# The adaLN columns of the last residual's gate, made in the feed-forward loop instead of beside the gate projections

## The chip, the cores and the metric

The kernel runs on one core of a Trainium2 chip, as one program. The metric is the device time of one execution in microseconds (us); where several executions were timed, their median is given. A profiled execution also has a span, from its first to its last instruction.

## The reference

One layer of a diffusion backbone works on 512 latent rows of width 1024, with 256 context rows beside them. The adaLN projection makes six vectors of 1024 values out of the condition `c`; the rest of the layer uses them as shift, scale and gate:

```python
ada = jax.nn.silu(c)[:, None, :] @ w_ada[layer] + b_ada[layer]
sh1, sc1, g1, sh2, sc2, g2 = jnp.split(ada, 6, axis=-1)
...
parts = _split_in(modulate(rms_norm(h_lat, norm1_w[layer]), sh1, sc1) @ w_in[layer])
mix, _ = _mixer(parts, lp, states, latent_conv)
h_lat = h_lat + g1 * mix
h_lat = h_lat + g2 * _swiglu(modulate(rms_norm(h_lat, norm2_w[layer]), sh2, sc2),
                             w_gate[layer], w_up[layer], w_down[layer])
return rms_norm(h_lat, final_norm_w)
```

`_mixer` joins a gated linear attention (GLA, 4 heads) and a state-space branch (SSD, 4 groups), `merged = sigmoid(gate_a) * y_a + sigmoid(gate_b) * y_b`, and multiplies the result by `w_out`. `_swiglu` has an inner width of 2816, that is 22 blocks of 128. All is float32. The gate `g2` is needed only at the very end, when the result of the feed-forward part is added to the residual.

## The kernel before

**Precision and weights.** Each float32 product is made of three matmuls, high x high, high x low and low x high. A weight block of 128 x 1024 values (512 KB) is loaded into one of three `raw` buffers by a transfer that SP issues (`load_raw`, L176), ScalarE copies it into the high half `whi_...` (L188), and VectorE, in some stages GpSimd (POOL), subtracts to get the low half `wlo_...` (L189). The high and the low halves have two buffers each. A raw buffer is free again when the low half is made. A scheduler sets the order of the instructions on each engine when the program is built; the engines then run their own lists in order and wait for each other through semaphores. SP runs no arithmetic: its list is that of the transfers.

**The adaLN columns.** `ada` holds 48 columns of 128 values, eight for each of the six vectors: 0 to 15 are made at the start, 16 to 23 are g1, 24 to 39 sh2 and sc2, 40 to 47 g2. `some_ada` makes the late ones beside other work. Every second call, as long as columns are left, it does two things: it finishes the column before (a matmul of a 128 x 128 block with a column of ones, L336, and a bias added by VectorE, L215) and starts the next (a load of 512 KB into a raw buffer, and on GpSimd a product with the condition, L341, two halvings, L343, and a last addition `apr`, L345). The calls stand in the projections of the GLA heads and, twice per step, in those of the gates.

**The stages in the text.** Before 880 us, the heads and the groups of the SSD. From about 880 to 990 us, the *gate stage*: a loop over the columns 2 to 7 of the merge gates (L927 on) loads and projects `ga_j` and `gb_j`, with `ya_j` read back from memory, while the recurrence of the last SSD group (`ssd_chain`) goes on: E row blocks are read from `cdr` (L829), biased (L830), multiplied by `cb` (L840), its outputs `y` are transposed (`yT`). The tanh of a gate, `tg`, is written to `tdr` by GpSimd's queue (L936). Then the rest of the columns, the row transpose `adaT` (L942), its copy `adT`, written to memory as `adr` by GpSimd's queue (L946) and read back by SP broadcast over the partitions: g1r (L949), sh2 and sc2 (L955). The last projection `pb_3` follows, and with it `merge` (L980 on), which reads `tgm` from `tdr` and for j below 2 `yam` from `ydr`, and adds on GpSimd (L989). The *output projection* (about 1008 to 1050 us) multiplies each `raw_out` by g1r on GpSimd (L187) and splits it. The norm `hn` (L1031, L1032) and its transposes `hT` (L1035) follow, while the first weights of the feed-forward part are split. The *feed-forward loop* (FFN; about 1070 to 1310 us) has 22 steps over the inner blocks, 48 matmuls each for `gate_j` and `up_j`; then w_down, the gate g2r and the last norm.

In the kernel before, `late` holds the columns 16 to 47, and g2r is read from the one `adr` at the start of the loop:

```python
while late or half_done:
    some_ada()
pt = sm_bank("adaT")
nc.tensor.transpose(pt[0:96, 0:P], ada.rearrange("p j t -> p (j t)"), ident)
```

Of the kernel before, what the change touches and what calls it, by code (L numbers as in the profile page):

```python
# [7 lines left out]
F32 = mybir.dt.float32  # L8
# [6 lines left out]
P = 128  # L15
D = 1024
# [113 lines left out]
def hybrid_layer_kernel(ctx: ExitStack, tc: tile.TileContext, x, xc, wts, vec, rows, up, msk, lvl, out):  # L130
    nc = tc.nc
# [10 lines left out]
    dr = ctx.enter_context(tc.tile_pool(name="dr", bufs=1, space=DRAM))  # L142

    def mm_bank(name):
        return ps.tile([P, 512], F32, tag="mm", name=name)

    def sm_bank(name):
        return ps.tile([P, 512], F32, tag="sm", name=name)
# [11 lines left out]
    ident = idt[:, :]  # L160
# [33 lines left out]
    def load_w(key, row=None):  # L194
        if key in ahead:
            return ahead.pop(key)
        nk, ncol = WSHAPE[key]
        nm = "_".join(map(str, key))
        hi = wp.tile([P, nk, ncol], F32R, tag="whi", name="whi_" + nm)
        lo = wp.tile([P, nk, ncol], F32R, tag="wlo", name="wlo_" + nm)  # L200
        return split_w(key, hi, lo, row)
# [9 lines left out]
    ada = cst.tile([P, 48, 2], F32, name="ada")  # L211
# [13 lines left out]
    with tc.tile_pool(name="st", bufs=1) as st:  # L225
# [77 lines left out]
        for i in range(6):  # L303
# [5 lines left out]
            for half in range(2):  # L309
                pt = sm_bank(f"xT_{i}_{half}")  # L310
# [11 lines left out]

    late = list(range(16, 48))
    half_done = []
    loads = [0]

# [137 lines left out]
    for d in range(2):  # L466
        for i in range(6):
            pt = sm_bank(f"pre_{d}_{i}")
# [16 lines left out]
    for b, i0, n in ((0, 0, 4), (1, 4, 2)):  # L485
        pt = sm_bank(f"dtT_{b}")
# [73 lines left out]
    for d in range(2):  # L560
        pt = sm_bank(f"cumT_{d}")
# [379 lines left out]
    pt = sm_bank("adaT")  # L941
# [5 lines left out]
    arow = adr.rearrange("(j t) p -> t j p", t=2)  # L947
# [66 lines left out]
    for i in range(4):  # L1014
# [14 lines left out]
        for half in range(2):  # L1029
# [3 lines left out]
            pt = sm_bank(f"hT_{i}_{half}")  # L1033
# [16 lines left out]
    fp = ctx.enter_context(tc.tile_pool(name="fp", bufs=1))  # L1050
    fH = fp.tile([P, NFF, SEQ], F32R, name="fH")
    fL = fp.tile([P, NFF, SEQ], F32R, name="fL")
    g2r = fp.tile([P, D], F32, name="g2r")
    nc.sync.dma_start(g2r.rearrange("p (j c) -> p j c", c=P), arow[0:1, 40:48, :].to_broadcast([P, 8, P]))
    fnr = fp.tile([P, D], F32, name="fnr")
    nc.sync.dma_start(fnr, rows[0:1, R_FN:R_FN + D].to_broadcast([P, D]))

    for j0, nj in [(0, 2)] + [(j, 1) for j in range(2, NFF)]:
        js = range(j0, j0 + nj)
        ws = {(key, j): load_w((key, j)) for j in js for key in ("gate", "up")}  # L1060
        pts = {(key, j): mm_bank(f"{key}_{j}") for j in js for key in ("gate", "up")}
        for t0, n in (((0, 256), (256, 256)) if nj == 2 else ((0, 512),)):
            tk = slice(t0, t0 + n)
            for kj, (hi, lo) in ws.items():
                for k in range(KD):
                    nc.tensor.matmul(pts[kj][:, tk], hi[:, k, :], h2H[:, k, tk], start=(k == 0), stop=False)  # L1066
                    nc.tensor.matmul(pts[kj][:, tk], hi[:, k, :], h2L[:, k, tk], start=False, stop=False)  # L1067
                    nc.tensor.matmul(pts[kj][:, tk], lo[:, k, :], h2H[:, k, tk], start=False, stop=(k == KD - 1))  # L1068
        for j in js:
            if nj == 2:  # L1070
                f = sml.tile([P, SEQ], F32, tag="snw", name=f"f_{j}", bufs=1)
            else:
                f = fp.tile([P, SEQ], F32, tag="f32", name=f"f_{j}", bufs=2)
            nc.scalar.activation(f, pts["gate", j], AF.Silu)
            nc.vector.tensor_tensor(f, f, pts["up", j], ALU.mult)  # L1075
            nc.scalar.activation(fH[:, j, :], f, AF.Copy)
            nc.vector.tensor_tensor(fL[:, j, :], f, fH[:, j, :].bitcast(F32), ALU.subtract)

    ob = [[(sm_bank if i < 2 else mm_bank)(f"db_{i}_{c}") for c in range(2)] for i in range(4)]
    fHk = [fH[:, k, :] for k in range(NFF)]  # L1080
    fLk = [fL[:, k, :] for k in range(NFF)]
    K0 = NFF - 6
# [119 lines left out]
```

## Time and profile before

| | |
|---|---|
| median of 3 runs | 1442.92 us (1441.3 to 1446.59) |
| profiled execution | 1443.79 us |
| its span | 1442.0 us, mean granted clock of TensorE 0.981 |
| TensorE matmuls busy | 1357.0 us (94% of the span) |
| VectorE busy | 882.6 us (61%) |
| ScalarE busy | 497.1 us (34%) |
| GpSimd busy | 475.3 us (33%) |

The first lines are times of whole executions; the others come from one profiled execution, that is from its span. TensorE is the engine with most work, and the time outside its 94% is either a wait at one of the stages or the start and the end of the kernel. The granted clock is the share of full speed (2.4 GHz) that TensorE was given; half of it, 1.2 GHz, is its other level. The program moves 175.48 MB in 1442.0 us.

### The profile page before, as it was taken

The numbers are of one execution on the slowest core, as the hardware profiler recorded it, in microseconds if no ns is written. First come the engines' busy times: TensorE is split into PE (matmuls) and PEld (weight loads), VectorE is DVE, ScalarE is ACT, GpSimd is POOL, SyncE is SP. The second block draws the span as 40 slices with busy tenths as digits, with TensorE's granted clock in tenths as the row PEclk, the third lists the DMA queues.
The fourth block names the chain that finished last, engine by engine and source line by source line (L and its number), as shares of the span: only waits on it lengthen the run. The fifth ranks groups of instructions, "written<-read, shape, count | busy, mean of one in ns | idle before, by whom it ended". The sixth has DMA issues, their size and how long they took to land.

```text
span 1442.0 us, 19130 instructions
## 1 busy us (share of the span) xinstructions
PE 1357.0 (94%) x7461; PEld 1149.3 (80%) x7461; DVE 882.6 (61%) x1316; ACT 497.1 (34%) x825; POOL 475.3 (33%) x340
## 2 busy tenths in 40 slices
PE   5989999999998999998999999999889999999997
PEld 3788999889888778877877787777678888888886
DVE  4699767573495588559757876785783333333235
ACT  6464333423434132523432342322233322322222
POOL 1346554344423533343353336445740000000001
PEclk9898999999999999999999999999999999999999
DMA  9385424433422432322322233558523222232331
GB/s 370 118 264 148 134 88 128 106 103 111 124 78 66 142 103 89 96 88 88 110 74 88 88 110 102 179 179 283 171 88 97 94 102 91 100 102 88 103 103 72
DMA packets 71354, 175.48 MB, mean 122 GB/s; under 512 B 6368, under 2 KB 22880, under 8 KB 71136
## 3 DMA queue, kind: packets, MB, share of 16 engines
q1 hardware_dynamic: 57056, 161.11, 33.5%
q0 software_dynamic: 13920, 12.78, 3.6%
q8 instruction: 59, 0.97, 0.3%
q10 hardware_dynamic: 288, 0.36, 0.1%
q14 instruction: 31, 0.25, 0.1%
HBM read 159.37 MB, written 14.86 MB: 121 GB/s over the span
## 4 chain that ended last, share of the span: by engine, by line
PE 62%; DVE 16%; DMA 11%; issue 5%; POOL 3%; ACT 2%; SPq 0%; POOLq 0%; DVEq 0%; ACTq 0%
DMA E<-cdr 7%; PE gate L1067 3%; PE gate L1068 3%; PE gate L1066 3%; PE up L1067 3%; PE up L1068 3%; PE up L1066 3%; PE db L206 3%; PE db L204 3%; PE db L205 3%; DVE E L830 2%; PE lv L577 2%; PE pb_pb L716 1%; PE pb_pb L715 1%; PE pb_pb L717 1%
## 5 line engine op out<-in xcount | busy, mean ns | idle before, releaser
L341 POOL TENSOR_TENSOR raw_ada<-raw_ada,cs 128x1024 f32<-128x1024 f32 x32 | 67.6, 2113 | 159.4 <-DMA raw_ada<-in_wts_dram 109.2
L170 POOL TENSOR_TENSOR rr_f<-rv_f,negh 128x1 f32<-128x1 f32 x4 | 2.6, 646 | 355.3 <-DVE rv_f L168 355.3
L830 DVE TENSOR_TENSOR E<-E,ebias 128x512 f32<-128x512 f32 x64 | 66.3, 1038 | 56.2 <-DMA E<-cdr 56.0
L386 PE MATMUL r_z<-whi_z,hH 128*128 128x256 f32 x256 | 74.5, 291 | 5.8 <-DVE cv_x L746 3.5
L343 POOL TENSOR_TENSOR raw_ada<-raw_ada 128x512 f32<-128x512 f32 x64 | 78.5, 1227 | 3.0
L388 PE MATMUL r_z<-whi_z,hL 128*128 128x256 f32 x256 | 73.2, 286 | 0.0
L387 PE MATMUL r_z<-wlo_z,hH 128*128 128x256 f32 x256 | 72.9, 285 | 0.0
L1067 PE MATMUL gate<-h2L,whi_gate 128*128 128x512 f32 (+1 forms) x192 | 72.0, 375 | 0.7 <-DVE h2L L1039 0.7
L1066 PE MATMUL gate<-h2H,whi_gate 128*128 128x512 f32 (+1 forms) x192 | 72.3, 377 | 0.0
L1068 PE MATMUL gate<-h2H,wlo_gate 128*128 128x512 f32 (+1 forms) x192 | 71.9, 374 | 0.0
L189 DVE TENSOR_TENSOR wlo_gate<-raw_gate,whi_gate 128x1024 fp32r<-128x1024 f32 x20 | 24.5, 1225 | 73.8 <-ACT whi_gate L188 73.8
L189 POOL TENSOR_TENSOR wlo_xs<-raw_xs,whi_xs 128x1024 fp32r<-128x1024 f32 x16 | 41.2, 2573 | 74.3 <-ACT whi_xs L188 74.3
L1066 PE MATMUL up<-h2H,whi_up 128*128 128x512 f32 x160 | 62.2, 389 | 0.0
L1067 PE MATMUL up<-h2L,whi_up 128*128 128x512 f32 x160 | 62.2, 389 | 0.0
L1068 PE MATMUL up<-h2H,wlo_up 128*128 128x512 f32 x160 | 62.2, 389 | 0.0
L189 DVE TENSOR_TENSOR wlo_down<-raw_down,whi_down 128x1024 fp32r<-128x1024 f32 x18 | 22.0, 1225 | 62.4 <-ACT whi_down L188 62.3
L833 ACT ACTIVATE E<-E 128x512 f32<-128x512 f32 x32 | 20.2, 632 | 112.0 <-DVE E L832 87.8
L1075 DVE TENSOR_TENSOR f<-f,up 128x512 f32<-128x512 f32 x22 | 15.1, 688 | 69.2 <-PE up L1068 68.5
L386 PE MATMUL r_v<-whi_v,hH 128*128 128x256 f32 x192 | 56.8, 296 | 0.0
L189 POOL TENSOR_TENSOR wlo_z<-raw_z,whi_z 128x1024 fp32r<-128x1024 f32 x16 | 39.7, 2484 | 49.1 <-ACT whi_z L188 39.4
L387 PE MATMUL r_v<-wlo_v,hH 128*128 128x256 f32 x192 | 55.8, 291 | 0.0
L388 PE MATMUL r_v<-whi_v,hL 128*128 128x256 f32 x192 | 55.8, 291 | 0.0
(475 smaller groups left out, 4544.4 us busy)
## 6 DMA issues: line engine op xcount, KB each, us to landing
raw_ada<-in_wts_dram SPq DMA_DIRECT2D x32, 512.0 KB, 4.0
E<-cdr SPq DMA_DIRECT2D x64, 256.0 KB, 3.6
raw_gate<-in_wts_dram SPq DMA_DIRECT2D x22, 512.0 KB, 3.5
raw_up<-in_wts_dram SPq DMA_DIRECT2D x22, 512.0 KB, 3.5
raw_down<-in_wts_dram SPq DMA_DIRECT2D x22, 512.0 KB, 3.5
aw<-in_wts_dram SPq DMA_DIRECT2D x8, 1024.0 KB, 15.5
raw_xs<-in_wts_dram SPq DMA_DIRECT2D x16, 512.0 KB, 3.5
raw_z<-in_wts_dram SPq DMA_DIRECT2D x16, 512.0 KB, 3.5
```

The lines of the kernel that those rows point to most:

```text
L189: (nc.gpsimd if split_pool[0] else nc.vector).tensor_tensor(lo, raw, hi.bitcast(F32), ALU.subtract)
L204: nc.tensor.matmul(out_, aH, bH, start=start, stop=False)
L205: nc.tensor.matmul(out_, aH, bL, start=False, stop=False)
L341: nc.gpsimd.tensor_tensor(raw, raw, cs[:, :, 0:1].to_broadcast([P, KD, P]), ALU.mult)
L343: nc.gpsimd.tensor_tensor(raw[:, 0:n, :], raw[:, 0:n, :], raw[:, n:2 * n, :], ALU.add)
L386: nc.tensor.matmul(o, hH[:, kk, tk], hi[:, k, :], start=st, stop=False, skip_group_check=True)
L387: nc.tensor.matmul(o, hH[:, kk, tk], lo[:, k, :], start=False, stop=False, skip_group_check=True)
L388: nc.tensor.matmul(o, hL[:, kk, tk], hi[:, k, :], start=False, stop=sp, skip_group_check=True)
L830: nc.vector.tensor_tensor(ed, ed, ebias[:, d, n, hh].unsqueeze(2).to_broadcast([P, EH, P]), ALU.add)
L1066: nc.tensor.matmul(pts[kj][:, tk], hi[:, k, :], h2H[:, k, tk], start=(k == 0), stop=False)
L1067: nc.tensor.matmul(pts[kj][:, tk], hi[:, k, :], h2L[:, k, tk], start=False, stop=False)
L1068: nc.tensor.matmul(pts[kj][:, tk], lo[:, k, :], h2H[:, k, tk], start=False, stop=(k == KD - 1))
```

## The change

The columns 40 to 47, those of g2, leave the list that is worked off beside the projections and the gates. The list gets them back ahead of the feed-forward loop, and each step of the loop from j = 2 on makes one call of `some_ada`, so that every second step makes a column. Behind the loop a row transpose of these eight columns alone (16 x 128) is made, copied, written to memory as `adr2` by GpSimd's queue and read back as g2r by SP. The arithmetic is the same.

```diff
@@ -322,7 +322,7 @@
 
 
 
-    late = list(range(16, 48))
+    late = list(range(16, 40))
     half_done = []
     loads = [0]
 
@@ -1050,14 +1050,15 @@
     fp = ctx.enter_context(tc.tile_pool(name="fp", bufs=1))
     fH = fp.tile([P, NFF, SEQ], F32R, name="fH")
     fL = fp.tile([P, NFF, SEQ], F32R, name="fL")
-    g2r = fp.tile([P, D], F32, name="g2r")
-    nc.sync.dma_start(g2r.rearrange("p (j c) -> p j c", c=P), arow[0:1, 40:48, :].to_broadcast([P, 8, P]))
+    late += range(40, 48)
     fnr = fp.tile([P, D], F32, name="fnr")
     nc.sync.dma_start(fnr, rows[0:1, R_FN:R_FN + D].to_broadcast([P, D]))
 
     for j0, nj in [(0, 2)] + [(j, 1) for j in range(2, NFF)]:
         js = range(j0, j0 + nj)
         ws = {(key, j): load_w((key, j)) for j in js for key in ("gate", "up")}
+        if j0 >= 2:
+            some_ada()
         pts = {(key, j): mm_bank(f"{key}_{j}") for j in js for key in ("gate", "up")}
         for t0, n in (((0, 256), (256, 256)) if nj == 2 else ((0, 512),)):
             tk = slice(t0, t0 + n)
@@ -1077,6 +1078,18 @@
             nc.vector.tensor_tensor(fL[:, j, :], f, fH[:, j, :].bitcast(F32), ALU.subtract)
 
     ob = [[(sm_bank if i < 2 else mm_bank)(f"db_{i}_{c}") for c in range(2)] for i in range(4)]
+    while late or half_done:
+        some_ada()
+
+    pt = sm_bank("adaT2")
+    nc.tensor.transpose(pt[0:16, 0:P], ada[:, 40:48, :].rearrange("p j t -> p (j t)"), ident)
+    adT2 = fp.tile([16, P], F32, name="adT2")
+    nc.vector.tensor_copy(adT2, pt[0:16, 0:P])
+    adr2 = dr.tile([16, P], F32, name="adr2")
+    nc.gpsimd.dma_start(adr2, adT2)
+    g2r = fp.tile([P, D], F32, name="g2r")
+    nc.sync.dma_start(g2r.rearrange("p (j c) -> p j c", c=P),
+                      adr2.rearrange("(j t) p -> t j p", t=2)[0:1].to_broadcast([P, 8, P]))
     fHk = [fH[:, k, :] for k in range(NFF)]
     fLk = [fL[:, k, :] for k in range(NFF)]
     K0 = NFF - 6
```

The scheduler places the moved instructions, and so the order on each engine changes at three places. The first is the transfer queue, SP, in the middle of the gate stage, from one raw_gb to the next. `raw_ada` is an adaLN column, `ya` the row block of the first branch, `E` the row blocks of the last SSD group. Before:

```order
L176 DMA raw_gb_4_8478<-in_wts_dram 128x1024
L176 DMA raw_ada_43_8514<-in_wts_dram 128x1024
L929 DMA ya_5_8509<-ydr_1127 128x512
L829 DMA E_3_2_1_1_8150<-cdr_700 128x512
L829 DMA E_3_3_0_0_8209<-cdr_700 128x512
L829 DMA E_3_3_0_1_8212<-cdr_700 128x512
L176 DMA raw_ga_5_8523<-in_wts_dram 128x1024
L176 DMA raw_gb_5_8557<-in_wts_dram 128x1024
```

And with the change, in the same stretch of the program:

```order
L176 DMA raw_gb_5_8520<-in_wts_dram 128x1024
L929 DMA ya_5_8482<-ydr_1127 128x512
L829 DMA E_3_2_1_1_8153<-cdr_700 128x512
L829 DMA E_3_3_0_0_8212<-cdr_700 128x512
L829 DMA E_3_3_0_1_8215<-cdr_700 128x512
L176 DMA raw_ga_6_8555<-in_wts_dram 128x1024
L829 DMA E_3_3_1_0_8220<-cdr_700 128x512
```

The raw_ada in front of ya and the three E is gone, and the weights are loaded one step further ahead: behind the same E stands raw_ga_6 where raw_ga_5 stood.

The second place is the end of the gate stage. On GpSimd (POOL), `adr` is the write of the row transpose, `tdr` that of a tanh, `tgm` the addition in the merge, `raw_out` the product of a weight block with g1r. Before:

```order
L343 TENSOR_TENSOR raw_ada_47_8759<-raw_ada_47_8759 128x256
L345 TENSOR_TENSOR apr_47_8764<-raw_ada_47_8759 128x128
L936 DMA tdr_1128<-tg_7_8710 128x1024
L989 TENSOR_TENSOR tgm_0_0_8829<-tgm_0_0_8829,tgm_0_1_8830 128x512
L946 DMA adr_8773<-adT_8771 96x128
L989 TENSOR_TENSOR tgm_1_0_8854<-tgm_1_0_8854,tgm_1_1_8855 128x512
L187 TENSOR_TENSOR raw_out_0_9025<-raw_out_0_9025,g1r_8775 128x1024
L187 TENSOR_TENSOR raw_out_1_9056<-raw_out_1_9056,g1r_8775 128x1024
L187 TENSOR_TENSOR raw_out_2_9087<-raw_out_2_9087,g1r_8775 128x1024
```

And with the change:

```order
L936 DMA tdr_1128<-tg_6_8584 128x1024
L170 TENSOR_TENSOR rr_y33_8265<-rv_y33_8263,negh_83 128x1
L946 DMA adr_8693<-adT_8691 96x128
L936 DMA tdr_1128<-tg_7_8653 128x1024
L989 TENSOR_TENSOR tgm_0_0_8749<-tgm_0_0_8749,tgm_0_1_8750 128x512
L989 TENSOR_TENSOR tgm_1_0_8774<-tgm_1_0_8774,tgm_1_1_8775 128x512
L187 TENSOR_TENSOR raw_out_0_8945<-raw_out_0_8945,g1r_8695 128x1024
L187 TENSOR_TENSOR raw_out_1_8976<-raw_out_1_8976,g1r_8695 128x1024
```

The write of adr now stands ahead of the last tdr and of tgm_0, where it stood behind both, and the columns' work in front of them is gone. On SP, in the same part of the program, `hres` are four blocks of the residual, 512 KB each. Before:

```order
L176 DMA raw_ada_47_8759<-in_wts_dram 128x1024
L176 DMA raw_pb_3_0_8811<-in_wts_dram 128x1024
L176 DMA raw_pb_3_1_8867<-in_wts_dram 128x1024
L176 DMA raw_pb_3_2_8917<-in_wts_dram 128x1024
L971 DMA hres_0_8795<-in_x_dram 128x1024
L971 DMA hres_1_8796<-in_x_dram 128x1024
L176 DMA raw_pb_3_3_8967<-in_wts_dram 128x1024
L971 DMA hres_2_8797<-in_x_dram 128x1024
L971 DMA hres_3_8798<-in_x_dram 128x1024
L176 DMA raw_out_0_9025<-in_wts_dram 128x1024
L986 DMA yam_1_8858<-ydr_1127 128x512
L176 DMA raw_out_1_9056<-in_wts_dram 128x1024
```

And with the change:

```order
L176 DMA raw_pb_3_2_8837<-in_wts_dram 128x1024
L986 DMA yam_0_8753<-ydr_1127 128x512
L982 DMA tgm_1_0_8774<-tdr_1128 128x512
L983 DMA tgm_1_1_8775<-tdr_1128 128x512
L176 DMA raw_pb_3_3_8887<-in_wts_dram 128x1024
L971 DMA hres_0_8715<-in_x_dram 128x1024
L971 DMA hres_1_8716<-in_x_dram 128x1024
L971 DMA hres_2_8717<-in_x_dram 128x1024
L971 DMA hres_3_8718<-in_x_dram 128x1024
L176 DMA raw_out_0_8945<-in_wts_dram 128x1024
L986 DMA yam_1_8778<-ydr_1127 128x512
L949 DMA g1r_8695<-adr_8693 128x8x128
```

The read of yam_1 follows the first raw_out in both; g1r, which stood behind the second raw_out and tgm_2_0, now follows yam_1 directly, and the last raw_pb stands ahead of all hres.

The third place is GpSimd at the end of the norm and the start of the feed-forward loop: `rr_h` are the roots of the norm, `hn_2_1` is half a block of the normalised rows, which is transposed afterwards. Before:

```order
L170 TENSOR_TENSOR rr_h1_9266<-rv_h1_9264,negh_83 128x1
L189 TENSOR_TENSOR wlo_gate_1_9415<-raw_gate_1_9416,whi_gate_1_9414 128x1024
L170 TENSOR_TENSOR rr_h2_9323<-rv_h2_9321,negh_83 128x1
L1032 TENSOR_TENSOR hn_2_1_9335<-hn_2_1_9335,sh2_1_8779 128x512
L170 TENSOR_TENSOR rr_h3_9380<-rv_h3_9378,negh_83 128x1
```

And with the change:

```order
L170 TENSOR_TENSOR rr_h1_9186<-rv_h1_9184,negh_83 128x1
L189 TENSOR_TENSOR wlo_gate_1_9335<-raw_gate_1_9336,whi_gate_1_9334 128x1024
L170 TENSOR_TENSOR rr_h2_9243<-rv_h2_9241,negh_83 128x1
L341 TENSOR_TENSOR raw_ada_40_9571<-raw_ada_40_9571,cs_85 128x1024
L1032 TENSOR_TENSOR hn_2_1_9255<-hn_2_1_9255,sh2_1_8699 128x512
L170 TENSOR_TENSOR rr_h3_9300<-rv_h3_9298,negh_83 128x1
L343 TENSOR_TENSOR raw_ada_40_9571<-raw_ada_40_9571 128x512
L343 TENSOR_TENSOR raw_ada_40_9571<-raw_ada_40_9571 128x256
L345 TENSOR_TENSOR apr_40_9576<-raw_ada_40_9571 128x128
```

The product of the first column, raw_ada_40, came to stand between rr_h2 and hn_2_1, and the rest of the column behind rr_h3. The other seven columns follow on GpSimd one after the other, with nothing between them.

## Rows read from the trace of the kernel before

**Rows 1.** Windows: bounds, length, busy us of PE, PEld, DVE, ACT, POOL; PEclk, DMA

```profile
880.00:990.00 110.00, 103.11 (x465) 80.03 (x465) 83.14 (x113) 29.97 (x48) 54.07 (x48) 0.98 0.51 170
...
1008.00:1050.00 42.00, 35.11 (x142) 27.03 (x141) 31.37 (x24) 12.24 (x15) 31.34 (x14) 0.96 0.52 168
...
1070.00:1310.00 240.00, 239.38 (x1146) 202.68 (x1147) 85.98 (x98) 71.10 (x93) 2.70 (x3) 0.99 0.28 92
```

**Rows 2.** Waits of TensorE (PE), 880 to 990 us: total, times, longest

```profile
PE l_gb L366 <- DVE wlo_gb L189: 2.9, 2, 2.5
PE l_gb L361 <- ACT whi_gb L188: 1.1, 1, 1.1
PE yi L577 <- DVE cb L842: 1.0, 1, 1.0
PE pb_pb L716 <- DVE yT L872: 0.9, 1, 0.9
PE ada L336 <- POOL apr L345: 0.9, 2, 0.7
```

**Rows 3.** Windows of 10 us around two waits, columns as in rows 1

```profile
930.00:940.00 10.00, 9.04 (x36) 7.32 (x37) 6.97 (x12) 4.78 (x9) 2.11 (x3) 0.83 0.86 290
...
1020.00:1030.00 10.00, 6.24 (x21) 4.68 (x20) 7.00 (x6) 2.21 (x3) 6.88 (x5) 0.83 0.42 130
```

**Rows 4.** Timeline of SP, POOL and DVE, 919 to 931 us: start, duration; idle before

```profile
919.92 8.17 SPq L829 DMA_DIRECT2D E<-cdr  x3
...
922.25 2.18 POOL L341 TENSOR_TENSOR raw_ada<-raw_ada,cs 128x1024 f32<-128x1024 f32 x1 [4.75 <-DVE xc_f L800]
...
924.57 1.42 DVE L830 TENSOR_TENSOR E<-E,ebias 128x512 f32<-128x512 f32 x1 [1.89 <-DMA E<-cdr]
...
929.69 1.21 DVE L189 TENSOR_TENSOR wlo_gb<-raw_gb,whi_gb 128x1024 fp32r<-128x1024 f32 x1
```

**Rows 5.** Timeline of VectorE (DVE) and GpSimd (POOL), one line at two times

```profile
886.62 1.29 DVE L840 TENSOR_TENSOR E<-E,cbs 128x512 f32<-128x512 f32 x2 [0.93 <-ACT cbs L838]
...
911.82 1.74 POOL L343 TENSOR_TENSOR raw_ada<-raw_ada 128x512 f32<-128x512 f32 x1
...
912.33 3.10 DVE L840 TENSOR_TENSOR E<-E,cbs 128x512 f32<-128x512 f32 x2
```

**Rows 6.** Waits of TensorE (PE), 1008 to 1050 us, columns as in rows 2

```profile
PE ob L205 <- DVE wlo_out L189: 5.2, 3, 3.8
```

**Rows 7.** Chain that ended last within 985 to 1030 us: start, duration

```profile
992.39 8.39 DMA yam<-ydr
```

**Rows 8.** Timeline of SP and POOL, 998 to 1014 us

```profile
998.90 0.38 SPq L949 DMA_DIRECT2D g1r<-adr  x1
...
1004.80 8.33 POOL L187 TENSOR_TENSOR raw_out<-raw_out,g1r 128x1024 f32<-128x1024 f32 x3 [1.01 <-DMA sh<-adr]
```

**Rows 9.** GpSimd's groups by line over the span: busy us, mean ns, idle before

```profile
L341 POOL TENSOR_TENSOR raw_ada<-raw_ada,cs 128x1024 f32<-128x1024 f32 x32 | 67.6, 2113 | 159.4 <-DMA raw_ada<-in_wts_dram 109.2 <-DVE eq L660 13.0 <-DVE ge L474 7.4
...
L343 POOL TENSOR_TENSOR raw_ada<-raw_ada 128x512 f32<-128x512 f32 x64 | 78.5, 1227 | 3.0
...
L345 POOL TENSOR_TENSOR apr<-raw_ada 128x128 f32<-128x128 f32 x32 | 21.7, 677 | 15.3 <-PE ada L336 15.2
```

**Rows 10.** Timeline of the feed-forward loop: SP, DVE, PE, ACT

```profile
1164.24 0.33 SPq L176 DMA_DIRECT2D raw_gate<-in_wts_dram  x1
...
1168.47 1.22 DVE L189 TENSOR_TENSOR wlo_gate<-raw_gate,whi_gate 128x1024 fp32r<-128x1024 f32 x1 [3.66 <-ACT whi_gate L188]
...
1173.25 0.39 PE L1068 MATMUL gate<-h2H,wlo_gate 128*128 128x512 f32 x1
...
1178.26 1.06 ACT L188 ACTIVATE whi_gate<-raw_gate 128x1024 fp32r<-128x1024 f32 x1 [3.84 <-PE gate L1067]
```

**Rows 11.** Timeline of GpSimd (POOL) and TensorE at the loop's start

```profile
1072.62 1.60 POOL L1032 TENSOR_TENSOR hn<-hn,sh 128x512 f32<-128x512 f32 x1 [2.03 <-DVE hn L1031]
...
1078.04 0.60 PE L1035 MATMUL hT<-idt,hn 128*128 128x128 f32 x4
```

## The prediction

> **What bounds the kernel now.** I read the stretches first. From 1070 us on, in the feed-forward (FFN) loop, TensorE is busy 239.38 of 240 us and GpSimd 2.70; from 880 to 990 us, where the last gate columns (ga, gb) are projected, TensorE is busy 103.11 of 110 and GpSimd 54.07; in the output projection, 1008 to 1050, it is busy 35.11 of 42 [rows 1]. So the FFN is pure TensorE time with an idle GpSimd, while the two stages around the moved work leave TensorE idle for 6.89 us each. Everything the kernel can win here is in those holes, and everything it can lose is a hole made where there is none.
>
> Then TensorE's own waits. In the gate stage there are seven, which make up 6.8 of the 6.89 us: two for the low half of a gb weight, 2.9 us together and the longer one 2.5; one each, of about 1 us, for the high half of a gb weight, for cb and for yT; two, 0.9 us together, for an adaLN column itself [rows 2]. A long wait costs more than itself: in the 10 us around it the granted clock is 0.83, where the neighbours have 1.00, so about a third of the stretch ran at the lower level, 1.2 GHz in place of 2.4, and about 1.7 us of work was lost ((1 - 0.83) x 10). The same 0.83 stands behind the long wait of the output projection [rows 3]. I count 6.9 + 1.7 = **8.6 us lost in each of the two stages**.
>
> Where the 2.5 us come from is in the timeline of the other engines. VectorE stood 1.89 us until an E row block had landed and reached the subtraction that TensorE wanted only at 929.69; the three E loads were issued from 919.92 on, behind raw_ada and ya on SP, and meanwhile GpSimd multiplied the raw column for 2.18 us [rows 4]. In that company VectorE itself is slow: two products of 128x512 take 1.29 us at one time, and 3.10 at another, while GpSimd adds the halves of a column [rows 5].
>
> **What goes away.** Columns 40 to 47 are not loaded in the gate stage: eight loads of 512 KB on SP, eight times the four GpSimd instructions. Per column these are 2.11 + 2 x 1.23 + 0.68 = 5.2 us [rows 9], so 42 of the stage's 54 busy us. Of the seven waits, the two for an adaLN column vanish with it. The 2.5 has its two causes (load and multiplication) removed; the 1.0 for cb [rows 2] comes behind two products on VectorE that a column on GpSimd holds up like those of [rows 5], and the 1.1 for the gb weight comes from a load that stands behind raw_ada. Not all of it must go: E still lands when it lands, and y, S_f and rr_y remain on GpSimd. I keep 1.5 us of the 8.6 as a remainder, between 0 (each wait was raw_ada's) and 4 (the 2.5 stays with its clock because E is late by itself). **Gain 7.0, from 4.5 to 8.6.** The TensorE pairs of the eight columns only change their place.
>
> **The output stage** starts from what GpSimd and SP do just before. Now g1r is asked for at 998.90, behind raw_out_1 and tgm_2_0, and the first three products of raw_out with g1r begin at 1004.80 [rows 8]; yam_1, issued at 992.39 in the middle of raw_pb, hres and raw_out, lands 8.39 us later [rows 7]. These two hold back the merge and the weights, and TensorE waits three times for a low half of w_out, 5.2 us together and 3.8 at once [rows 6]. In the new order adr stands before tgm_0 on GpSimd, g1r directly behind yam_1 on SP, and the four raw_pb are loaded before the hres, since no raw buffer is held by columns 46 and 47. From the rows: tgm_0 comes when the last gate is through, that is some 7 us earlier like TensorE itself; g1r no longer waits for raw_out_1 and tgm_2_0 and is issued about 998.9 - 992.4 = 6.5 us earlier on top of that. GpSimd then starts on raw_out when tgm_1 is done, limited by yam_1, so I give the chain 4 us relative to TensorE, not 6.5. That covers the wait of 3.8 us and with it, nearly, its clock, 1.7: **gain 5.0**; lower bound 0 (TensorE simply arrives 7 us earlier at a chain that moved by as much), upper 8.6. In the stretch behind it, up to 1078 us, where hn and the splits of the first FFN weights meet on VectorE and GpSimd, nothing is removed; I leave it as it is, with 2 us either way for a pattern that shifts.
>
> **What is added in the FFN.** Eight columns at 5.2 us, one per two steps of the loop. A step is 48 matmuls, some 10 us (1146 of them in 240 us [rows 1]). The subtraction of the next gate weight ends at 1169.69 and TensorE wants it at 1173.25: 3.56 us of cover [rows 10]. One instruction of GpSimd in front of it is at most 2.11 by its mean, so VectorE is late by less than the cover. On TensorE a column costs one 128x1 matmul in place of one before. SP: the load asked for at 1164.24 is copied by ScalarE at 1178.26, 14 us later with some 4 us to land; a third buffer lent to raw_ada for about 4 + 5.2 us moves a load by one place, half a step or 5 us, and that fits into the 10 us of cover. In the first of them, GpSimd's multiplication of raw_ada_40 stands before hn_2_1, which now runs at 1072.62; its transposes are at 1078.04 on TensorE [rows 11], so 1078.04 - 1072.62 - 1.60 = 3.8 us cover the 2.1. The row transpose adaT2, adr2 and g2r are made some 140 us before g2r is used in the last rows of the kernel; one transpose on TensorE, 0.3 us. raw_up_19 queues behind g2r on SP and has the same 10 us. **Cost 0.5, from 0 to 2**; if the cover were gone, each column would cost what VectorE is late.
>
> The Trainium skill speaks against this part: the page "SBUF — State Buffer", section "SBUF: two separate sides", says that VectorE with two SBUF operands and GpSimd take one port pair as an exclusive lock, whoever comes first for the whole instruction, and the other is blocked. The 3.10 against 1.29 us [rows 5] agrees. By that rule a subtraction in the FFN waits for at most the one instruction in progress, which the cover above hides, so the sum would be the same; if the lock were won by GpSimd several times running, rival 2 below.
>
> **Sum.** 1443.8 (the profiled execution, span 1442.0) - 7.0 - 5.0 + 0.5 = 1432.3. The median of the runs is 0.9 lower than the profiled one, so **1431.5 us**. Its own range: 1443.8 - 8.6 - 8.6 - 2 = 1424 at the best, 1443.8 - 4.5 - 2 + 0.5 = 1438 at the worst.
>
> **Rivals.**
> 1. *The output stage keeps its waits.* If yam_1 lands as late relative to TensorE as now, only the gate stage is won: 1443.8 - 7 + 0.5 - 0.9 = 1436.4. For it: hres is still 2 MB ahead of yam_1 on SP, and GpSimd's eight products with g1r (8.33 us for three [rows 8]) remain. Against it: g1r is earlier by more than TensorE. Chance 0.22.
> 2. *GpSimd stalls the FFN* (the other side). Place: the subtraction of wlo_gate or wlo_up while a column is being made. If all four instructions come before it, VectorE is late by 5.2 us, 1.7 over the cover, eight times: 13 us, and 1460 if the clock drops 1.7 with each. Then the time is 1443.8 - 12 + 13 = 1445 to 1459. It decides from 12/8 = 1.5 us per column on. For it: VectorE is held for 1.8 us by a single neighbour [rows 5]. Against it: wlo_gb at 929.69 took 1.21 just after such a block, and in the gate stage, where VectorE is 76% busy (83.14 of 110) beside the same columns, no wait is longer than 2.5. Chance 0.08.
> 3. *New waits take the place of the old ones.* E rows are late by themselves (VectorE waits for their landing, 1.89 [rows 4]), TensorE comes early to an unready yT or hn, and only 2 to 4 us are left: 1439 to 1441. It needs the 2.5 to be E's fault alone. Chance 0.15.
>
> **How the numbers follow.** The forecast has 0.55. A measurement of this kernel, with runs from 1441.3 to 1446.6, can tell about 0.5% or 7.2 us from no change, so faster means under 1435.7. Of the forecast nine tenths lie there, of rival 1 two fifths, of rival 3 none: 0.50 + 0.09 = 0.59. Slower, above 1450.1, is half of rival 2 and a little for mishaps: 0.06. The rest, 0.35, is the same. The range goes from 1424 to 1441, which takes in rivals 1 and 3.
>
> **What would show it.** After the change: no raw_ada between 868 and 985 us and GpSimd's busy time there down by some 42 us; the wait for wlo_gb under 1 us and the clock at 1.00 in all of the gate stage; TensorE reaching the transpose adaT some 7 us earlier; g1r landed before tgm_1 is added, and the largest wait of the output stage under 2 us; FFN stretches with TensorE idle under 0.2 us per step, even where a column is made, and wlo_gate there of up to 3 us instead of 1.22. I am wrong if a wait over 2 us for E, hn or w_out stands again in the gate or output stage (rivals 1, 3), or if the FFN steps with a column are longer than those without (rival 2).

## The result and the profile after

The changed kernel takes **1431.87 us** (median of 4 runs, 1428.55 to 1432.8) against 1444.73 us before (4 runs, 1441.3 to 1446.59): a ratio of 0.991 with a 95% interval of 0.9882 to 0.9937. Timed again beside the first experiments, it took 1432.36 us, ratio 0.9904 (0.9883 to 0.9924). Its profiled execution took 1428.55 us, with a span of 1426.7.

The windows of the changed kernel that answer to [rows 1], columns as there, each placed inside the same stage, which ends 15 to 16 us earlier now; the second one holds the whole output stage, where that of [rows 1] holds 42 us of it:

```profile
870.00:980.00 110.00, 110.00 (x500) 86.35 (x499) 75.82 (x115) 32.17 (x51) 23.02 (x23) 1.00 0.49 162
992.00:1044.00 52.00, 45.90 (x189) 35.93 (x188) 37.43 (x32) 16.62 (x24) 34.45 (x16) 0.97 0.47 149
1060.00:1300.00 240.00, 240.00 (x1146) 202.35 (x1146) 93.48 (x101) 71.35 (x90) 40.77 (x33) 1.00 0.36 112
```

In the gate stage TensorE never stops: 110.00 of 110 us, where it was 103.11, with GpSimd at 23.02 in place of 54.07. In the loop it does not stop either, though GpSimd now works 40.77 us there. The output stage is little better: it is idle for 6.10 of 52 us, where it was for 6.89 of 42. The waits of TensorE from 880 to 1110 us, which answer to [rows 2, 6]; columns: total, times, longest:

```profile
PE hT L1035 <- DVE hn L1032: 4.7, 1, 4.7
PE ob L205 <- DVE wlo_out L189: 3.4, 2, 2.4
PE ob L204 <- ACT whi_out L188: 1.4, 2, 0.8
PE ob L204 <- ACT w L188: 1.4, 1, 1.4
```

Nothing of [rows 2] is left; of the output stage's waits [rows 6] the longest is 2.4 us in place of 3.8, but all of them together are 6.1 us where they were 6.8.

So that a stage can be compared between runs whose stages begin at other times, I took the stretches between fixed matmuls, by the start times on TensorE's timeline: "GLA" from the last `l_q` to the last `r_v`, "gate" from the last `r_z` to the first `ob`, "out" to the first `hT`, "norm" to the first `gate`, "loop" to the first `db`, "end" to the last matmul. In brackets the waits that the rows in the stretch name; the wait of a stretch's first matmul is named with it, though it lies in the time of the stretch before. All later tables are made like this, one profiled execution each, in us:

| kernel | GLA | gate | out | norm | loop | end |
|---|---|---|---|---|---|---|
| before | 43.2 (2.9) | 148.6 (6.8) | 51.9 (6.8) | 8.3 (4.0) | 245.5 (0.7) | 119.8 |
| before, second profile | 38.8 (0.7) | 154.0 (10.6) | 52.2 (9.2) | 7.9 (3.9) | 246.3 (0.9) | 119.8 |
| changed | 38.7 (0.7) | 136.1 (0) | 52.3 (6.1) | 8.2 (4.7) | 246.3 (0) | 119.8 |
| changed, second profile | 38.7 (0.7) | 136.1 (0) | 52.7 (6.4) | 8.0 (4.4) | 246.1 (0) | 119.8 |

Of the 15.3 us between the first two spans, 12.5 were won in the gate stage, 4.5 in a stretch that the change does not touch (GLA, which the second profile of before shows at 38.8), and 1.2 were given back in the output stage and the loop; the stretches not listed make up the rest. By the gate stage's matmuls, each from its start to the next start, the 12.5 are: waits 6.8; the clock behind the 2.5 us wait 1.7 (from 931.0 to 934.4 us it was granted at 0.50, and nowhere else in the stage under 1.00); the columns' own matmuls 1.9; the remaining 2.1 are longer matmuls next to interleaved small ones and behind waits, most of them in l_gb, which takes 36.5 us before and 33.5 now with that clock in it. The matmuls of the columns are in the loop now, where they and the longer matmuls next to them cost about as much.

### The profile page after: what moved, and what is told of

It is laid out like the page before. It is cut to its first block, busy times and chain, and to the rows that moved or that the text cites. A ratio compares the mean times of both kernels' runs of the same rounds, so it can differ in the third digit from the quotient of the medians.

```text
span 1426.7 us, 19130 instructions
## 1 busy us (share of the span) xinstructions
PE 1349.4 (95%) x7462; PEld 1146.0 (80%) x7462; DVE 881.1 (62%) x1317; ACT 496.7 (35%) x825; POOL 476.1 (33%) x341
## 4 chain that ended last, share of the span: by engine, by line
PE 66%; DVE 16%; DMA 9%; issue 5%; ACT 2%; POOL 1%; SPq 0%; POOLq 0%; DVEq 0%; ACTq 0%
DMA E<-cdr 6%; PE up L1069 3%; PE gate L1068 3%; PE gate L1069 3%; PE up L1068 3%; PE gate L1067 3%; PE up L1067 3%; DVE E L830 3%; PE db L204 3%; PE db L206 3%; PE db L205 3%; PE lv L577 2%; PE pb_pb L716 2%; PE pb_pb L715 2%; PE pb_pb L717 2%
## 5 line engine op out<-in xcount | busy, mean ns | idle before, releaser
L189 DVE TENSOR_TENSOR wlo_gate<-raw_gate,whi_gate 128x1024 fp32r<-128x1024 f32 x20 | 31.7, 1584 | 45.6 <-ACT whi_gate L188 45.6
L715 PE MATMUL pb_pb<-yT,whi_pb 128*128 128x512 f32 x128 | 55.3, 434 | 0.0
L205 PE MATMUL db<-wlo_down,fH 128*128 128x512 f32 x142 | 55.3, 389 | 0.0
```

The costliest lines, as they stand in the source:

```text
L189: (nc.gpsimd if split_pool[0] else nc.vector).tensor_tensor(lo, raw, hi.bitcast(F32), ALU.subtract)
L205: nc.tensor.matmul(out_, aH, bL, start=False, stop=False)
L715: nc.tensor.matmul(pt, hi[:, k, cl], aH[:, k, :], start=(k == 0), stop=False)
```

## Experiments

My theory after the result: GpSimd's work on the columns held up VectorE in the gate stage, and that alone was the gain; the loads of w_ada, the other cause that I had named, may have had no part. The output stage is held by something that an earlier start doesn't help. All kernels start from the changed one; each ratio is to runs of the kernel before that were taken together with it.

**GpSimd's work alone, back in the gate stage.**

```diff
+    dum = sml.tile([P, 4, P], F32, name="dumt", bufs=1)
+    nc.gpsimd.memset(dum, 0.0)
...
         nc.sync.dma_start(ya, ydr[:, j, :])
+        for _ in range(2):
+            nc.gpsimd.tensor_tensor(dum, dum, ya.rearrange("p (k c) -> p k c", k=4), ALU.mult)
+        for n in (4, 2, 1):
+            nc.gpsimd.tensor_tensor(dum[:, 0:n, :], dum[:, 0:n, :], dum[:, 0:n, :], ALU.add)
         lat, _ = proj_cols(("ga", j), False)
```

> The changed kernel, with GpSimd work of the size of a column put back into the gate stage once per step (two products of 128x512, additions of 512, 256 and 128 columns on a scratch tile that nothing else uses, 5 to 6 us per step), but no load of w_ada and no TensorE column there. If the waits of the gate stage came from GpSimd holding VectorE, TensorE idles 2 to 5 us again between the first gate projection and the output projection and the kernel loses 3 to 6 us against the changed one (some 1435 to 1438). If they came from the loads on SP alone, idle stays under 0.5 us and the time is that of the changed kernel, 1432.

**Loads alone, back in the gate stage.**

```diff
+    dum = [sml.tile([P, 1], F32, name="dumt", bufs=1)]
+    def dummy_column(j):
+        raw = load_raw(("ada", j))
+        nc.gpsimd.tensor_copy(dum[0], raw[:, 0, 0:1])
...
         if key[0] in ("ga", "gb"):
             some_ada()
+            if key[0] == "ga" and key[1] >= 2:
+                dummy_column(38 + key[1])
```

> The changed kernel, with six loads of 512 KB of w_ada put back into the gate stage, one per step ahead of the ga weight, each taking a raw buffer; GpSimd reads one value per row of each, 128x1, and nothing more is made of them. If the loads (SP's order, the raw buffer) were the cause, TensorE idles 3 to 6 us in the gate stage and the time is 1435 to 1440. If GpSimd's work was, idle stays under 1 us and the time is 1432 to 1433.

And twelve of them in place of six (the condition on "ga" dropped):

> As the kernel with loads alone in the gate stage, but twelve loads of 512 KB there in place of six, two per step; GpSimd reads one value per row of each. If loads cost the stage 0.8 us as the first run's profile shows, twice as many cost 1 to 3 us and TensorE idles under 2 us: stage of 137 to 139 us, time of 1434. If loads and their buffers are a cause of their own, the stage is 5 us longer or more: 1438 and above.

The kernel before, once more:

> The kernel before itself, for a second profile: gate stage (last r_z to the first output matmul) again 148 to 149 us with 6 to 8 us of TensorE's waits for wlo_gb, whi_gb, cb, yT and the columns. If the 2.5 us wait was a chance of one execution, the stage is 3 us shorter.

| kernel | GLA | gate | out | norm | loop | end | median | ratio to before |
|---|---|---|---|---|---|---|---|---|
| GpSimd's work alone | 38.7 | 147.0 (7.3) | 52.8 | 7.7 | 246.2 | 119.8 | 1445.14 | 1.000 (0.9981 to 1.002) |
| six loads alone | 42.8 | 136.9 (0) | 52.3 | 7.7 | 247.7 | 123.2 | 1437.62 | 0.9953 (0.9928 to 0.9978) |
| twelve loads alone | 42.6 | 139.7 (2.3) | 52.5 | 9.1 | 245.9 | 123.1 | 1443.59 | 0.9984 (0.9967 to 1.0002) |

The work on GpSimd alone takes the whole gain away, 12.8 us against the changed kernel timed with it, 10.9 of them in the gate stage: more than I had expected, and with less work than the columns were (GpSimd is busy for 54.77 us of the stage, where it was for 64.91 before and is for 24.60 in the changed kernel; the windows stand further down). The waits of TensorE in that stage, in this kernel:

```profile
PE l_gb L361 <- ACT whi_gb L188: 1.6, 1, 1.6
PE l_gb L366 <- DVE wlo_gb L189: 1.5, 3, 0.6
PE y L577 <- DVE E L840: 1.5, 1, 1.5
PE pb_pb L715 <- ACT yT L871: 1.3, 1, 1.3
PE pb_pb L717 <- POOL wlo_pb L189: 1.3, 1, 1.3
```

They stand at other places than before, but they are of the same kind: a result of VectorE, or of ScalarE, comes a little too late. ScalarE, for one, has E ahead of the whi_gb for which TensorE waits 1.6 us, and VectorE took 1.24 us for its last step on that E beside the scratch work. It had stood 2.5 us for the row to land before, although no column is loaded here. The last wait is GpSimd's own: wlo_pb stands behind two scratch products in its list. The second profile of before, too, has other waits than the first, among them 3.2 us for yT and 3.0 for whi_gb, and none of 2.5 for wlo_gb; I had expected a stage of 148 to 149 us, and it was 154.0. So the place of a wait changes from execution to execution, and the stage's length tells more.

Six loads leave TensorE no wait at all. They are felt on VectorE, though. Its waits for E rows in the gate stage, in the kernel before, the changed one, that with six loads and that with twelve (total, times, longest; with the tile alone, below, they are 4.7 us together):

```profile
DVE E L830 <- DMA E<-cdr: 9.5, 6, 3.4
DVE E L830 <- DMA E<-cdr: 4.5, 5, 1.6
DVE E L838 <- DMA E<-cdr: 6.9, 6, 2.5
DVE E L838 <- DMA E<-cdr: 12.4, 7, 4.0
```

More loads make E come later; with six, TensorE's cover hides it. The time, however, lay 5 us above the changed kernel's, and the table shows that this was not the gate stage's: the last stage is 3.4 us longer, without a wait, far from any load. So one more run had to tell the loads from the tile of four bytes that I had added for them.

**The tile alone.**

```diff
+    dum = sml.tile([P, 1], F32, name="dumt", bufs=1)
+    nc.gpsimd.memset(dum, 0.0)
     def some_ada():
```

> The changed kernel with one more tile of four bytes per partition, filled once and used by nothing, at the place where the two kernels with loads alone have theirs; no loads, no work in the gate stage. In those two the last matmuls of w_down take 396 ns in place of 389 with no wait and the full clock, and their last stage is 3.4 us longer. If that comes from the tile, which moves the tiles behind it by four bytes, the last stage is 123 us again (119.8 in the changed kernel), the time is some 1436 to 1438 and the gate stage stays at 136 us. If it comes from the loads, the last stage is 119.8 us and the time 1432.

| kernel | GLA | gate | out | norm | loop | end | median | ratio to before |
|---|---|---|---|---|---|---|---|---|
| tile alone | 42.7 | 136.9 (0) | 53.0 | 7.9 | 246.5 | 123.1 | 1442.24 | 0.9963 (0.9946 to 0.998) |

It is the tile. The costliest group of the last stage in this kernel, and then in the changed one (after the bar: busy us, mean ns of one):

```profile
L205 PE MATMUL db<-wlo_down,fH 128*128 128x512 f32 x140 | 55.4, 396 | 0.0
```

```profile
L205 PE MATMUL db<-wlo_down,fH 128*128 128x512 f32 x140 | 54.5, 389 | 0.0
```

The same matmuls take 396 in place of 389 ns, and the last stage is 3.3 us longer; the time is above the 1436 to 1438 that I had expected. Against this kernel as the base, six loads cost the gate stage nothing (136.9 both), and twelve 2.8 us. So the loads do not make the waits of before by themselves. Whether the later E rows add to a wait while GpSimd holds VectorE as well, and what it costs that a real column keeps its raw buffer until GpSimd has added it up (here it is free after one value per row), no run shows. The tile's slower matmuls are in the times of the two kernels with loads, and I draw nothing from those times.

**What the columns cost in the loop.** Without them (one line, `late += range(40, 48)`, is dropped; the last gate is zero), and twice over:

> The changed kernel without the columns 40 to 47 at all: they are left at zero, so the last gate is zero; row transpose, adr2 and g2r stay. If the columns cost the feed-forward loop only their sixteen TensorE instructions, the loop is 1.5 to 2 us shorter and the time is 1430. If GpSimd's work beside VectorE had cost the loop stalls, it is 5 us shorter or more.

```diff
-    late += range(40, 48)
+    late += list(range(40, 48)) * 2
...
         if j0 >= 2:
             some_ada()
+            some_ada()
```

> The changed kernel with the columns 40 to 47 made twice over in the feed-forward loop, one per step in place of one per two steps: 16 loads, 80 instructions of 41 us more on GpSimd. If a column costs only its TensorE pair, 0.24 us, the loop is 2 us longer and stays without waits of TensorE: 1434. If GpSimd beside VectorE or the lent raw buffers stall the loop once the columns stand close together, TensorE waits in the loop and it is 5 to 15 us longer.

| kernel | GLA | gate | out | norm | loop | end | median | ratio to before |
|---|---|---|---|---|---|---|---|---|
| no columns of g2 | 38.6 | 136.1 (0) | 52.7 | 8.0 | 243.5 (0) | 119.8 | 1430.02 | 0.9893 (0.9868 to 0.9918) |
| columns twice | 43.1 | 136.1 (0) | 52.4 | 8.0 | 249.5 (1.0) | 119.8 | 1433.62 | 0.9905 (0.9879 to 0.993) |

With the eight columns the loop is 2.6 to 2.8 us longer, without a wait; with eight more another 3.3, with one wait of 1.0 us for a column itself. Not all of the first is the columns': the loop begins in a stretch at the lower clock behind the wait for hn. Its first 5 us, in the changed kernel and then without columns (columns as in [rows 1]), are granted 0.65 and 0.86, which is 1.0 us of the difference:

```profile
1052.80:1057.80 5.00, 4.96 (x28) 4.67 (x28) 4.93 (x8) 1.82 (x5) 2.42 (x2) 0.65 0.00 0
1056.05:1061.05 5.00, 4.95 (x35) 4.66 (x35) 4.93 (x9) 1.82 (x5) 2.06 (x2) 0.86 0.00 0
```

The rest is what the TensorE pair and the slower matmul behind it take. GpSimd's hold on VectorE is there all the same. The timeline of the changed kernel in a step that makes a column:

```profile
1118.24 0.28 PE L336 MATMUL ada<-one,apr 128*128 128x1 f32 x2
1118.38 0.48 PE L1069 MATMUL up<-h2H,wlo_up 128*128 128x512 f32 x1
...
1118.43 1.91 POOL L341 TENSOR_TENSOR raw_ada<-raw_ada,cs 128x1024 f32<-128x1024 f32 x1 [16.68 <-DMA raw_ada<-in_wts_dram]
...
1118.70 0.39 PE L1067 MATMUL up<-h2H,whi_up 128*128 128x512 f32 x1
...
1118.89 2.52 DVE L189 TENSOR_TENSOR wlo_gate<-raw_gate,whi_gate 128x1024 fp32r<-128x1024 f32 x1 [0.18 <-ACT whi_gate L188]
...
1124.53 1.23 DVE L189 TENSOR_TENSOR wlo_up<-raw_up,whi_up 128x1024 fp32r<-128x1024 f32 x1
```

From start to start the pair takes 0.14 us, and the matmul behind it 0.32 where the next one takes 0.23: 0.23 us per column, 1.8 for eight. The subtraction of wlo_gate takes 2.52 us beside the product on GpSimd, and that of wlo_up 1.23 when GpSimd is through; the first ends 1.3 us late, with 3.56 us of cover [rows 10].

**The output stage.** Three edits: the merge's additions on VectorE (`nc.gpsimd` to `nc.vector` in L989), the products with g1r left out (the two lines of L186 and L187 dropped), and the gate g1 applied behind the projection:

> The changed kernel with the eight additions of the merge in the output stage on VectorE in place of GpSimd. If the output stage is held by GpSimd's queue (its products with g1r and the merge together), TensorE's 6.1 us of waits there fall to 2 or less and the kernel gains 4 to 6 us: 1427. If it is held by the transfers of tgm and of raw_out or by VectorE, nothing is gained: 1431 to 1434.

> The changed kernel without the products of w_out with g1r on GpSimd: the gate g1 is left out of the computation. If these products, through GpSimd's queue and through VectorE that they hold, are what keeps TensorE waiting in the output stage, the waits there fall from 6.1 us to under 2 and the kernel is 4 to 7 us faster: 1426. If the merge is what holds it, waits of 4 us or more stay.

```diff
-        hi, lo = load_w(("out", k), g1r)
+        hi, lo = load_w(("out", k))
...
+            nc.vector.tensor_tensor(ob[i][c], ob[i][c], g1r[:, cl], ALU.mult)
             nc.vector.tensor_tensor(hres[i][:, cl], hres[i][:, cl], ob[i][c], ALU.add)
```

> The changed kernel with the gate g1 applied behind the output projection, by eight products of 128x512 on VectorE in the accumulator, in place of the eight products of w_out blocks with g1r on GpSimd. If those products hold the output stage, it shrinks from 52.5 to about 46 us, as it did with g1 left out, while the norm behind it gets 8 x 0.68 us more on VectorE, of which 1 to 3 us show: 1428. If VectorE's longer way to hn eats it all, 1432 or more.

And one for the wait of the norm, with `split_pool` left false for the first weights of the loop:

> The changed kernel with the four low halves of the first feed-forward weights made by VectorE in place of GpSimd. The 4.7 us wait of TensorE for hn stands where VectorE is held by those subtractions on GpSimd. If that is its cause, the wait falls to 2 us and the kernel gains 2 to 5 us with the clock: 1428. If VectorE's own work is the cause, four more instructions of 1.2 us on it make the wait longer: 1434 to 1437.

| kernel | GLA | gate | out | norm | loop | end | median | ratio to before |
|---|---|---|---|---|---|---|---|---|
| merge on VectorE | 38.6 | 136.1 (0) | 51.4 (4.9) | 8.6 (4.8) | 246.7 | 119.8 | 1431.27 | 0.9907 (0.9874 to 0.994) |
| no products with g1r | 38.8 | 136.1 (0) | 45.7 (0.8) | 8.6 (6.0) | 246.0 | 119.8 | 1424.81 | 0.9857 (0.9807 to 0.9907) |
| g1 at the residual | 43.4 | 136.1 (0) | 48.4 (1.5) | 9.8 (9.0) | 248.1 (0.6) | 119.8 | 1430.64 | 0.9882 (0.9861 to 0.9903) |
| first splits on VectorE | 42.8 | 136.1 (0) | 52.8 (6.3) | 5.6 (2.7) | 249.3 (1.6) | 119.8 | 1435.54 | 0.992 (0.9887 to 0.9953) |

The merge's additions on GpSimd are not what holds the stage: moved to VectorE, they give 1 us, and the waits only change their names. The products with g1r are: without them the stage is 6.6 us shorter and TensorE waits 0.8 (that kernel doesn't wait for g1r itself either, but g1r had already come early). The timeline of the changed kernel shows how, across the engines:

```profile
995.08 6.19 POOL L187 TENSOR_TENSOR raw_out<-raw_out,g1r 128x1024 f32<-128x1024 f32 x2
...
996.12 2.88 DVE L988 SCALAR_TENSOR_TENSOR tgm<-tgm,acc_b 128x512 f32<-128x512 f32 x1
...
998.93 2.88 DVE L991 SCALAR_TENSOR_TENSOR mt<-tgm,mt 128x512 fp32r<-128x512 f32 x1
...
1001.84 0.32 SPq L983 DMA_DIRECT2D tgm<-tdr  x1
...
1004.58 1.28 DVE L988 SCALAR_TENSOR_TENSOR tgm<-tgm,acc_b 128x512 f32<-128x512 f32 x1 [2.76 <-DMA tgm<-tdr]
...
1005.78 1.21 DVE L189 TENSOR_TENSOR wlo_out<-raw_out,whi_out 128x1024 fp32r<-128x1024 f32 x1
...
1007.04 0.50 PE L205 MATMUL ob<-wlo_out,mt 128*128 128x512 f32 x1 [2.41 <-DVE wlo_out L189]
```

While GpSimd makes two products, two instructions of VectorE take 2.88 us each in place of 0.68. So the buffer of the merge comes free late, the next tgm is asked for at 1001.84, VectorE stands 2.76 us for it with the subtraction of wlo_out queued behind, and TensorE waits 2.41 us for that. The longest wait of before [rows 6] came by the same steps:

```profile
1018.47 2.67 DVE L991 SCALAR_TENSOR_TENSOR mt<-tgm,mt 128x512 fp32r<-128x512 f32 x1 [0.15 <-ACT mt L990]
...
1021.16 0.33 SPq L983 DMA_DIRECT2D tgm<-tdr  x1
...
1023.83 1.31 DVE L988 SCALAR_TENSOR_TENSOR tgm<-tgm,acc_b 128x512 f32<-128x512 f32 x1 [2.69 <-DMA tgm<-tdr]
...
1026.33 0.64 PE L205 MATMUL ob<-wlo_out,mt 128*128 128x512 f32 x1 [3.76 <-DVE wlo_out L189]
```

An earlier start of the chain doesn't change any of these steps.

Taking the products off GpSimd and putting them on VectorE behind the projection gives 4 us of the stage, less than the 6.5 expected, and loses them again at the norm and the start of the loop: TensorE's waits for hn grow to 9.0 us. Moving the first splits to VectorE shortens the norm by 2.4 us, as it should if GpSimd held VectorE there, but lengthens the loop's start by 3. Neither kernel's time can be told from the changed one's.

## Why the prediction was right, and where it was not

The time came out as forecast, 1431.87 for 1431.5, and the main cause was the one named. But two terms of the sum were off by about 5 us each, one way and the other; that the total fits so well is luck. One bound of the range doesn't follow from its terms either: 1438 at the worst takes 2 us of gain from the output stage, whose lower bound is 0. With 0 there, and the loop's cost at its 2, the sum is 1441.3, and 1443.3 with the 2 us for a pattern that shifts.

**Gate stage, 7.0 us: right in its cause, too small.** It was 12.5 (17.9 against the second profile of before). The waits and their clock went whole, 6.8 and 1.7 us, so that no remainder stayed where I had kept 1.5. The other 4 us are matmul time for which the sum had nothing: 1.9 of the columns' own matmuls, which only moved, as I had put them down, and come back in the loop, and 2.1 of longer matmuls around them and behind waits. Of the two causes that I gave for the 2.5 us wait, the experiments show one to be enough: GpSimd's work brings 7.3 us of waits back by itself (none longer than 1.6), the loads alone none. They do not clear the other, the late E row for which VectorE stood 1.89 us [rows 4]: E rows come later with more loads, but one was 2.5 us late without any. In the second profile of before VectorE doesn't stand for E ahead of the same subtraction, and TensorE's wait there is 1.7 us in place of 2.5.

How much of this GpSimd does by holding VectorE, and how much by its own late y and S_f behind the column, was not separated. For the 3.0 us wait for whi_gb in the second profile of before, the rows show the first:

```profile
972.77 1.91 POOL L341 TENSOR_TENSOR raw_ada<-raw_ada,cs 128x1024 f32<-128x1024 f32 x1 [6.75 <-DMA raw_ada<-in_wts_dram]
...
972.97 2.25 DVE L857 TENSOR_TENSOR y<-y,yi 128x512 f32<-128x512 f32 x1
...
978.16 0.60 ACT L864 ACTIVATE y<-y 128x512 f32<-128x512 f32 x1 [7.95 <-DVE ada L215]
...
978.79 1.04 ACT L188 ACTIVATE whi_gb<-raw_gb 128x1024 fp32r<-128x1024 f32 x1
```

Beside the product, VectorE's addition to y takes 2.25 us in place of 0.69, and two instructions beside the halvings lose another 0.8; ScalarE, which has y ahead of whi_gb in its list, stands until VectorE is through with y and with ada, the short instruction behind it. Other rows show the hold too. The eight products of line L840 in the gate stage, before, after, and with GpSimd's work put back (after the bar: busy us, mean ns):

```profile
L840 DVE TENSOR_TENSOR E<-E,cbs 128x512 f32<-128x512 f32 x8 | 10.5, 1351 | 1.5 <-ACT cbs L838 1.5
```

```profile
L840 DVE TENSOR_TENSOR E<-E,cbs 128x512 f32<-128x512 f32 x8 | 5.2, 687 | 1.2 <-ACT cbs L838 1.2
```

```profile
L840 DVE TENSOR_TENSOR E<-E,cbs 128x512 f32<-128x512 f32 x8 | 6.6, 864 | 0.0
```

Half of their time was GpSimd's before; with the work put back, other instructions bear more of it. Over all its lines VectorE was busy 84.50 us for this stretch before, and 72.27 after, for nearly the same instructions; with GpSimd's work put back, 82.23. The windows of the three kernels, columns as in [rows 1], before first, then the changed one, then that with the work put back:

```profile
868.00:985.00 117.00, 111.06 (x495) 85.67 (x494) 84.50 (x114) 29.77 (x48) 64.91 (x54) 0.99 0.47 154
```

```profile
864.00:972.00 108.00, 108.00 (x488) 84.34 (x487) 72.27 (x110) 31.56 (x50) 24.60 (x24) 1.00 0.44 143
```

```profile
868.00:983.00 115.00, 110.32 (x484) 84.31 (x482) 82.23 (x110) 31.01 (x49) 54.77 (x50) 0.99 0.43 138
```

**Output stage, 5.0 us: wrong; it lost 0.4.** The step that failed is "that covers the wait of 3.8 us and with it, nearly, its clock". The chain did start earlier: the first two products with g1r, which answer to [rows 8], stand at 984.02:

```profile
984.02 6.19 POOL L187 TENSOR_TENSOR raw_out<-raw_out,g1r 128x1024 f32<-128x1024 f32 x2
```

That is 20.8 us earlier than 1004.80, where TensorE was 16.4 us earlier at the stage's first matmul, so the lead was 4.4, near the 4 that I gave it. But the stage isn't limited by its start. GpSimd stood for the next addition of the merge, which needs TensorE's last projection, before it could go on:

```profile
993.83 1.29 POOL L989 TENSOR_TENSOR tgm<-tgm,tgm 128x512 f32<-128x512 f32 x1 [3.62 <-DVE tgm L988]
```

And each step on the way from product to weight takes as long as before, since the products hold VectorE. The 3.8 us wait had been such a step, a read of tgm asked for late, and not the late g1r and yam_1 to which I had put it down. By the prediction's own sign this part was wrong: a wait of over 2 us for w_out stands there again, 2.4 us, and one of 4.7 for hn behind it. The first rival had this right, for the other reason that it gave: the eight products on GpSimd remain. Its time, 1436.4, was off by what the gate stage gave in addition.

**Loop, cost 0.5: about right.** Between the profiles of before and after the loop differs by 0.8; leaving the columns out takes 2.6 to 2.8 off it, of which 1.8 are the moved matmuls and 1.0 the clock at its start. The cover held as worked out: wlo_gate took 2.52 us of the 3 that I allowed, no wait followed. The second rival's point, 1.5 us per column, was far off: 0.23, and 0.4 with a column in every step, a wait of 1.0 us included. raw_ada_40 ahead of hn_2_1 did nothing that shows; the norm is as long as before, and g2r was asked for at 1247.7 for a first use near 1398.

**New waits (third rival): none in the gate stage.** The yT and the E were in time for TensorE as soon as GpSimd was out of the way, though VectorE still stood 4.5 us for E.

## What to carry to other kernels

Side work on GpSimd is not free where VectorE feeds the engine that sets the pace: look for a stage in which VectorE has a few us of cover per step, and put it there; the price in this one was the matmuls of the side work itself. A chain that starts earlier shortens a stage only if the start is what limits it; leave out the work suspected of setting its rhythm and see whether the stage shrinks before counting on it. And when an experiment adds a tile, run the tile alone.

## What the runs showed of the hardware

**Which of two engines is held can decide 4 us.** The stretch "GLA" is 38.6 to 38.8 us in some profiles and 42.6 to 43.4 in others; both profiles of before, from the same program, have one of each. The timeline at its fork, in the first profile of before (43.2 us):

```profile
310.09 2.15 POOL L341 TENSOR_TENSOR raw_ada<-raw_ada,cs 128x1024 f32<-128x1024 f32 x1 [2.53 <-DMA raw_ada<-in_wts_dram]
...
310.39 2.39 DVE L667 TENSOR_TENSOR ek<-ek,kv 128x512 f32<-128x512 f32 x1
...
312.71 1.75 DVE L660 TENSOR_TENSOR eq<-eq,qT 128x512 f32<-128x512 f32 x1
...
312.93 1.85 PE L577 MATMUL lv<-eq,ek 128*128 128x128 f32 x8 [1.92 <-DVE ek L667]
```

And in the second (38.8 us):

```profile
311.98 3.94 POOL L341 TENSOR_TENSOR raw_ada<-raw_ada,cs 128x1024 f32<-128x1024 f32 x1 [2.55 <-DMA raw_ada<-in_wts_dram]
...
312.25 0.69 DVE L667 TENSOR_TENSOR ek<-ek,kv 128x512 f32<-128x512 f32 x1
...
312.86 0.69 DVE L660 TENSOR_TENSOR eq<-eq,qT 128x512 f32<-128x512 f32 x1
```

In the first GpSimd's product took 2.15 us, and two of VectorE's instructions, one beside the product and one beside the addition that follows, took 2.39 and 1.75 us in place of 0.69. In the second VectorE's went at 0.69 one after the other, and GpSimd's product took 3.94 us. In the first, TensorE then waited 1.9 us for ek, and the granted clock of 310 to 320 us fell to 0.66, where it is 1.00 in the second. All 14 profiles go one of these two ways, seven each, and the stretch is the long one in just the seven where VectorE was held. The starts on record do not tell which way it goes: in all 14 GpSimd's product starts 0.05 to 0.31 us before VectorE's ek. The Trainium skill's page "SBUF — State Buffer", section "SBUF: two separate sides", calls the shared port pair an exclusive lock that whoever starts first keeps for its whole instruction. These rows agree that one of the two is held, with the loser on either side; that the first to start wins, they do not show.

**A tile of four bytes slowed matmuls that do not use it.** With one more tile of 128x1 in a pool, filled once and read by nothing, the last stage's matmuls took 396 ns in place of 389 at a granted clock of 1.00 and without waits; that stage was 3.3 us longer and the gate stage 0.8, also without a wait. The first experiment's tile of 2 KB per partition did no such thing. By the ratios, 0.9963 against 0.9904 and 0.991, the kernel was some 8 us slower. The GLA stretch stood at its longer time in all three profiles with the tile, but it does so in four of the eleven without it too, so how much of the 8 us is the tile's beyond the 4 of these two stages is not shown. Which of the tiles moved, and what their place changes for TensorE, was not found out.
